# DeltaNet side tasks: order edges behind the latest dense unit, longer pauses behind loads and powers

## The chip, the cores and the metric

The kernel runs on one core of one Trainium2 chip. The metric is the device time of one execution in microseconds, as the median of several runs. The core has five engines that run side by side, each through its own list of instructions in order: TensorE (PE in the profile, its weight loads PEld), VectorE (DVE), ScalarE (ACT), GpSimd (POOL) and SyncE (SP), which issues most of the DMAs.

## The reference

A trunk of two layers on 528 tokens (16 meta tokens and 512 others) of width 1024: forgetting attention, a convolutional feed-forward block, gated DeltaNet, and a second feed-forward block. The change touches DeltaNet alone. Cut to what matters:

```python
def gated_deltanet(h, w_in, conv_w, a_log, dt_bias, o_gain, w_out):
    proj = hp @ w_in
    qkv, og, b_logit, a_logit = jnp.split(proj, ...)
    qkv = jax.nn.silu(causal_dwconv(qkv, conv_w))
    q = l2norm(q) * (Dh ** -0.5); k = l2norm(k)
    beta = jax.nn.sigmoid(b_logit)
    gc = jnp.cumsum(g, axis=-1)                      # per chunk
    dec = jnp.exp(gc[..., :, None] - gc[..., None, :])   # lower triangle
    A = jnp.where(strict, (k k^T) * dec * beta, 0.0)
    sol = triangular_solve(A + I, [k * beta * exp(gc), v * beta])
    W, U0 = sol
    qk = (q k^T) * dec
    def step(S, xs):                                 # over the chunks
        U = U0_n - W_n S
        O = qd_n S + qk_n U
        S = gl_n * S + U^T kd_n
        return S, O
    O = rmsnorm(O, o_gain) * jax.nn.silu(og)
    return O @ w_out
```

8 heads of 128 elements; the kernel uses chunks of 16, 128, 128, 128 and 128 tokens.

## The kernel before

**Dense units.** Every weight matrix is cut into units of 128 output columns. `dense` (L297 to L318) multiplies one unit with one of two halves of the tokens (272 and 256), in three products per 128 input rows (high and low parts of both sides): 24 matmuls for a unit of 1024 rows, all on L312. `push` runs the second half of a unit four units later. After its matmuls a unit has its own work on other engines: `conv_tile` takes the sums off PSUM on DVE (L748), convolves on DVE and ACT (L755, L764); `og` does the gate (L1388, L1390); `part` copies a partial output (L871).

**Tasks.** Around the dense units DeltaNet runs its recurrence in groups of two heads (g = 0 to 3). Each group has generator tasks: `kchain` makes the decays (`decays`, L1044: DVE on a row `gcr` that SP loads), the Gram matrices of K (`gram_k`: sums L1020 and products L1075 on PE, a power on POOL L1063, the matrix AT by DVE L1082), the small inverse of the first chunk (`solve_meta`, L1129), and `solve`. `solve` sends AT through DRAM (`dA`, `AB`), does 31 steps of substitution on POOL (L1177 and L1178 per step, on the tile RB), sends the result through DRAM again (`dR`, then `Rc`), and finishes the inverse with copies (L1192), a transposition (L1189) and small matmuls (L1199 to L1236). `qchain` does the same for Q. `schain` runs `scan`, chunk by chunk: transposes (L1256, L1257) and K·S (L1260) on PE, VB (ACT L1262, DVE L1265), inverse times VB (PE L1270), U (ACT L1272), U times KD (PE L1277), the new state S (DVE L1281 or L1283), and the output (PE L1289, L1291; ACT L1296, L1297). `heads_out` then norms the output: MO on DVE (L1308), a power on POOL (L1309), OU times MO on POOL (L1312), transposes on PE (L1316), and the copy to O.

**What sets the order.** `Flow` keeps a planned time `now`, which `dense` moves on by 0.33 for every three matmuls; a task that yields a number sleeps for that much planned time, one that yields a condition until it holds. `tick`, called inside `dense`, steps the tasks that are due. So the constants T_... set where a task's instructions stand among the dense matmuls. PE keeps that order for the dense matmuls and for those of `scan` (`tok`); what stands where on DVE, ACT and POOL is decided by a scheduler with its own estimates. Before a new K, Q or V tile `hd_tile` looks whether 16 of them are in use; if so, `flow.until` steps tasks until a scan has freed six, and no dense matmul is recorded meanwhile. In program order this falls 595 dense matmuls behind the first transpose of L952 (the start of the tasks); the last unit of DeltaNet ends at 1549. At the end `flow.until` runs the tasks that are left. A group's `decays` wait for the scan of the group two before; its `solve` waits for the substitution of the group before.

Of the kernel before, what the change touches and what calls it, by code (L numbers as in the profile page):

```python
# [9 lines left out]
F32 = mybir.dt.float32  # L10
# [3 lines left out]
ALU = mybir.AluOpType  # L14
# [19 lines left out]
T_BLOCKS = 4  # L34
T_STEP = 0.5
T_INV = 10
T_OUT = 3.5
# [67 lines left out]
def trunk(ctx, tc, h0, wflat, params, out):  # L105
# [110 lines left out]
    class Flow:  # L216
# [11 lines left out]
        def step(self, t):  # L228
            self.busy = True
            try:  # L230
                r = next(t["gen"])
            except StopIteration:
                self.tasks.remove(t)
                r = None
            self.busy = False
            t["cond"] = None
            if callable(r):
                t["cond"] = r
            elif r is not None:
                t["wake"] = self.now + r  # L240
# [496 lines left out]
    def conv_tile(u, half, ft, taps, base, stride, pool, carry):  # L737
# [4 lines left out]
        with tc.high_priority(offset=300):  # L742
# [5 lines left out]
            nc.vector.tensor_tensor(ub[:, c0:c0 + n], ps, r[:, :n], op=ALU.mult)  # L748
# [6 lines left out]
            nc.scalar.activation(cv, ub[:, c0:c0 + n], AF.Identity, scale=w[c0])  # L755
# [85 lines left out]
    def deltanet(layer, post, pre, wcx):  # L841
# [21 lines left out]
        def part(u, half, mt):  # L863
            n = HALF[half][1] - (CUT if half == 0 else 0)
            if mt == 0:
                drop(*X[half][:2])
                m[half] = take(half, "m", shape=[P, KT, n])
                OHL[half] = split(half, 0)
            x = OHL[half]
            ps = dense(u, half, lambda k: x[:, 0, k, :], lambda k: x[:, 1, k, :], 0, n)  # L870
            nc.vector.tensor_copy(m[half][:, mt, :], ps)  # L871
            if mt == 7:
                drop(x)
                OHL[half] = None

        with ExitStack() as cx:
# [3 lines left out]
            flow.on = False  # L880
        HALF[0] = (CUT, 272 - CUT)
# [17 lines left out]
    def dn_heads(layer, O, cx, part):  # L899
# [81 lines left out]
        def group(g):  # L981
# [47 lines left out]
            def decays(half):  # L1029
                s, n = HALF[half]  # L1030
                if half == 0:
# [4 lines left out]
                    st["QDm"] = dp.tile([16, NG, 16], F32, name="QDm", tag="QDm", bufs=2)  # L1036
                for hl in range(NG):
                    hd = g * NG + hl
                    gcr = dp.tile([P, 272], F32, name="gcr", tag="gc", bufs=2)
                    nc.sync.dma_start(gcr[:, :n], gcd[hd:hd + 1, s:s + n].to_broadcast([P, n]))  # L1040
# [11 lines left out]
            def gram_k(half):  # L1052
# [10 lines left out]
                nc.gpsimd.tensor_tensor(rk[:, cs, :], y[:, cs, :], mhalf[:, 0:w * NG].rearrange("p (c x) -> p c x", x=NG), op=ALU.pow)  # L1063
                nc.vector.tensor_tensor(rho[:, cs, :], y[:, cs, :], rk[:, cs, :], op=ALU.mult)
# [19 lines left out]
            def gram_q(half):  # L1084
# [9 lines left out]
                yield T_HOP  # L1094
                pgs = [psum_tile("g") for _ in range(NG)]
# [5 lines left out]
                for hl in range(NG):  # L1101
# [6 lines left out]
                    eg = dp.tile([P, 272], F32, name="eg", tag="gc", bufs=2)  # L1108
                    nc.sync.dma_start(eg[:, :n], gcd[hd:hd + 1, s:s + n].to_broadcast([P, n]))
# [45 lines left out]
            def solve():  # L1155
# [18 lines left out]
                for l in range(31):  # L1174
# [3 lines left out]
                    nc.gpsimd.tensor_tensor(R3[:, 0:a, l + 1:32], R3[:, 0:a, l + 1:32], t, op=ALU.subtract)  # L1178
# [125 lines left out]
            def heads_out(ci, OU, MO):  # L1304
# [8 lines left out]
                yield 0.0  # L1313
# [24 lines left out]
            def kchain(half):  # L1338
                yield lambda: ("gates", half) in done and (g < 2 or ("scan", g - 2) in done)
                decays(half)  # L1340
# [40 lines left out]
        def og(u, half, hd):  # L1381
# [98 lines left out]
```

## Time and profile before

| | |
|---|---|
| median of 3 runs | 1604.69 us (1602.89 to 1607.8) |
| the profiled execution's own time | 1601.35 us |
| its span (first to last instruction) | 1599.4 us |
| busy in the span | PE 95%, DVE 70%, ACT 51%, POOL 31% |
| mean granted TensorE clock | 0.977 |

The profile's span leaves 1.95 us of the execution outside it. Busy shares are over the whole kernel; the change touches the stretch from about 825 to 1172 us, in which PE runs dense units and tasks in turn.

### The profile page before, as it was taken

The numbers are of one execution on the slowest core, as the hardware profiler recorded it, in microseconds if no ns is written. First come the engines' busy times: TensorE is split into PE (matmuls) and PEld (weight loads), VectorE is DVE, ScalarE is ACT, GpSimd is POOL, SyncE is SP. The second block draws the span as 40 slices with busy tenths as digits, with TensorE's granted clock in tenths as the row PEclk, the third lists the DMA queues.
The fourth block names the chain that finished last, engine by engine and source line by source line (L and its number), as shares of the span: only waits on it lengthen the run. The fifth ranks groups of instructions, "written<-read, shape, count | busy, mean of one in ns | idle before, by whom it ended". The sixth has DMA issues, their size and how long they took to land.

```text
span 1599.4 us, 33295 instructions
## 1 busy us (share of the span) xinstructions
PE 1525.8 (95%) x12630; PEld 1486.8 (93%) x12630; DVE 1123.4 (70%) x2629; ACT 815.4 (51%) x1925; POOL 495.8 (31%) x993
## 2 busy tenths in 40 slices
PE   8999999999999999999789899899989999999996
PEld 6999999899999999999789798898989999999996
DVE  7888888948974675674978665676569864765764
ACT  6677777735643442343564456545456543432441
POOL 6434443025300010012556475654154200100112
PEclk9999999999999999999799998999999999999998
DMA  5232222422223222222323322222141323323321
GB/s 175 89 89 79 75 78 85 134 65 82 84 83 100 93 85 88 93 93 72 107 75 90 90 61 71 68 77 61 50 150 66 91 82 106 92 82 106 93 67 53
DMA packets 63327, 139.04 MB, mean 87 GB/s; under 512 B 18584, under 2 KB 31288, under 8 KB 62784
## 3 DMA queue, kind: packets, MB, share of 16 engines
q1 hardware_dynamic: 62544, 134.55, 28.1%
q8 instruction: 99, 1.62, 0.4%
q0 software_dynamic: 480, 2.15, 0.4%
q14 instruction: 60, 0.49, 0.1%
q10 hardware_dynamic: 144, 0.22, 0.0%
HBM read 131.54 MB, written 5.36 MB: 86 GB/s over the span
## 4 chain that ended last, share of the span: by engine, by line
PE 74%; DVE 11%; POOL 5%; DMA 4%; ACT 3%; issue 3%; SPq 1%; POOLq 0%; DVEq 0%; ACTq 0%
PE ps L312 65%; POOL PR L1177 2%; POOL RB L1178 2%; DVE h L412 1%; DVE bt L411 1%; DVE wl L292 1%; PE av L698 1%; DMA w<-wflat 1%; DVE cv L764 1%; DMA gcr<-gcd 1%; PE pt L678 1%; DVE xl L378 1%; ACT wh L285 1%; PE s L1277 1%; DVE qr L577 1%
## 5 line engine op out<-in xcount | busy, mean ns | idle before, releaser
L312 PE MATMUL ps<-xh,wh 128*128 128x256 f32 (+4 forms) x2464 | 717.6, 293 | 16.8 <-DVE ub L748 9.2
L312 PE MATMUL ps<-xl,wh 128*128 128x256 f32 (+4 forms) x2464 | 710.8, 289 | 3.4 <-DVE xl L378 3.0
L312 PE MATMUL ps<-xh,wl 128*128 128x256 f32 (+4 forms) x2464 | 713.6, 290 | 0.0
L312 PEld LDWEIGHTS ps<-xh,wh 128*128 128x128 f32 (+1 forms) x2464 | 469.6, 192 | 22.8 <-DVE ub L748 6.3
L312 PEld LDWEIGHTS ps<-xl,wh 128*128 128x128 f32 (+1 forms) x2464 | 471.1, 191 | 7.4 <-DVE xl L378 4.6
L312 PEld LDWEIGHTS ps<-xh,wl 128*128 128x128 f32 (+1 forms) x2464 | 471.1, 191 | 1.0
L285 ACT CAST wh<-w 128x1024 fp32r<-128x1024 f32 (+3 forms) x226 | 225.1, 997 | 189.5 <-PE ps L312 166.7
L292 DVE TENSOR_TENSOR wl<-w,wh 128x1024 fp32r<-128x1024 f32 (+4 forms) x191 | 220.6, 1156 | 99.3 <-ACT wh L285 98.7
L764 DVE SCALAR_TENSOR_TENSOR cv<-ub,prm,cv 128x256 f32<-128x256 f32 (+2 forms) x494 | 243.8, 498 | 38.4 <-ACT cv L755 29.5
L312 PE MATMUL ps<-ah,wl 128*128 128x256 f32 (+2 forms) x704 | 199.5, 284 | 0.0
L312 PE MATMUL ps<-ah,wh 128*128 128x256 f32 (+2 forms) x704 | 199.3, 283 | 0.0
L312 PE MATMUL ps<-al,wh 128*128 128x256 f32 (+2 forms) x704 | 199.1, 283 | 0.0
L755 ACT ACTIVATE cv<-ub,prm 128x256 f32<-128x256 f32 (+2 forms) x224 | 113.8, 511 | 146.3 <-DVE ub L748 146.2
L748 DVE TENSOR_TENSOR ub<-ps,r 128x256 f32<-128x256 f32 (+2 forms) x224 | 95.4, 428 | 101.5 <-PE ps L312 100.6
L353 POOL TENSOR_TENSOR ssq<-ssq,sq 128x256 f32<-128x256 f32 (+2 forms) x98 | 90.5, 926 | 144.5 <-ACT sq L352 143.0
L312 PEld LDWEIGHTS ps<-ah,wh 128*128 128x128 f32 x704 | 132.6, 189 | 0.0
L312 PEld LDWEIGHTS ps<-al,wh 128*128 128x128 f32 x704 | 132.5, 188 | 0.0
L312 PEld LDWEIGHTS ps<-ah,wl 128*128 128x128 f32 x704 | 132.4, 188 | 0.0
L751 POOL COPY cy<-ub 128x2 f32<-128x2 f32 (+1 forms) x112 | 38.0, 341 | 279.3 <-DVE ub L748 277.7
L292 POOL TENSOR_TENSOR wl<-w,wh 128x512 fp32r<-128x512 f32 x70 | 95.0, 1377 | 72.1 <-ACT wh L285 56.8
L747 POOL COPY ub<-cy 128x2 f32<-128x2 f32 (+1 forms) x112 | 31.3, 280 | 197.1 <-DVE cv L764 160.0
L786 ACT ACTIVATE gl<-cv 128x272 f32<-128x272 f32 (+2 forms) x88 | 36.7, 418 | 42.0 <-DVE cv L764 41.7
(308 smaller groups left out, 2454.5 us busy)
## 6 DMA issues: line engine op xcount, KB each, us to landing
w<-wflat SPq DMA_DIRECT2D x176, 512.0 KB, 3.5
w<-wflat SPq DMA_DIRECT2D x32, 448.0 KB, 3.3
cB<-cdram SPq DMA_DIRECT2D x16, 264.0 KB, 3.3
w<-wflat SPq DMA_DIRECT2D x16, 256.0 KB, 2.7
h<-h SPq DMA_DIRECT2D x8, 272.0 KB, 5.3
cB<-cdram SPq DMA_DIRECT2D x16, 136.0 KB, 3.0
h<-h SPq DMA_DIRECT2D x8, 256.0 KB, 5.0
AB<-dA SPq DMA_DIRECT2D x16, 128.0 KB, 3.2
```

The source lines that it names most:

```text
L285: nc.scalar.copy(wh[:], w32)
L292: eng.tensor_tensor(wl[:, c], w32[:, c], wh[:, c].bitcast(F32), op=ALU.subtract)
L312: tok(nc.tensor.matmul(o, w[:, a], r[:, c0:c1], start=(i == 0), stop=(i == tot - 1)))
L353: nc.gpsimd.tensor_tensor(self.acc[:, :n], self.acc[:, :n], sq[:, :n], op=ALU.add)
L747: nc.gpsimd.tensor_copy(ub[:, 0:c0], carry.pop(ft)[:, :c0])
L748: nc.vector.tensor_tensor(ub[:, c0:c0 + n], ps, r[:, :n], op=ALU.mult)
L751: nc.gpsimd.tensor_copy(c[:, :c0], ub[:, n:n + c0])
L755: nc.scalar.activation(cv, ub[:, c0:c0 + n], AF.Identity, scale=w[c0])
L764: nc.vector.scalar_tensor_tensor(cv, ub[:, i:i + n], w[i], cv, op0=ALU.mult, op1=ALU.add)
L786: nc.scalar.activation(g, cv, AF.Gelu_apprx_tanh)
L1177: nc.gpsimd.tensor_tensor(t, R3[:, 0:a, l:l + 1].to_broadcast([P, a, w]), A3[:, l:l + 1, l + 1:32].to_broadcast([P, a, w]), op=ALU.mult)
L1178: nc.gpsimd.tensor_tensor(R3[:, 0:a, l + 1:32], R3[:, 0:a, l + 1:32], t, op=ALU.subtract)
```

## The change

A dictionary `anchors` keeps, for an engine, the latest instruction of a dense unit (DVE L748, L871, L1388; ACT L755, L1390) and the latest subtraction of the substitution (POOL L1178). While a task is stepped, each instruction that it records gets an edge behind the anchor of its engine. The constants are set anew: a pause T_LOAD stands between the loads of `gcr` or `eg` and their use, T_POW behind the power of `gram_k`, T_BACK between the load of `Rc` and its first use; T_BLOCKS, T_STEP, T_INV and T_OUT have other values, and `heads_out` pauses T_OUT + 1 before its transposes in place of 0.

```diff
-T_BLOCKS = 4
-T_STEP = 0.5
-T_INV = 10
-T_OUT = 3.5
+T_BLOCKS = 8
+T_LOAD = 3.5
+T_POW = 2
+T_STEP = 0.9
+T_BACK = 5.5
+T_INV = 2.5
+T_OUT = 2
...
         def step(self, t):
             self.busy = True
-            try:
-                r = next(t["gen"])
-            except StopIteration:
-                self.tasks.remove(t)
-                r = None
+            with ExitStack() as es:
+                for i in anchors.values():
+                    es.enter_context(tc.issue_after(i))
+                try:
+                    r = next(t["gen"])
+                except StopIteration:
+                    self.tasks.remove(t)
+                    r = None
...
+    anchors = {}
+
+    def anchor(engine, inst):
+        if flow.on:
+            anchors[engine] = inst.ins
...
-            nc.vector.tensor_tensor(ub[:, c0:c0 + n], ps, r[:, :n], op=ALU.mult)
+            anchor("dve", nc.vector.tensor_tensor(ub[:, c0:c0 + n], ps, r[:, :n], op=ALU.mult))
...
-            nc.scalar.activation(cv, ub[:, c0:c0 + n], AF.Identity, scale=w[c0])
+            anchor("act", nc.scalar.activation(cv, ub[:, c0:c0 + n], AF.Identity, scale=w[c0]))
...
+                gcrs = []
                 for hl in range(NG):
                     hd = g * NG + hl
-                    gcr = dp.tile([P, 272], F32, name="gcr", tag="gc", bufs=2)
-                    nc.sync.dma_start(gcr[:, :n], gcd[hd:hd + 1, s:s + n].to_broadcast([P, n]))
+                    gcrs.append(dp.tile([P, 272], F32, name="gcr", tag="gc", bufs=2))
+                    nc.sync.dma_start(gcrs[hl][:, :n], gcd[hd:hd + 1, s:s + n].to_broadcast([P, n]))
+                yield T_LOAD
...
                 nc.gpsimd.tensor_tensor(rk[:, cs, :], y[:, cs, :], mhalf[:, 0:w * NG]..., op=ALU.pow)
+                yield T_POW
...
-                    nc.gpsimd.tensor_tensor(R3[:, 0:a, l + 1:32], R3[:, 0:a, l + 1:32], t, op=ALU.subtract)
+                    anchor("pool", nc.gpsimd.tensor_tensor(R3[:, 0:a, l + 1:32], R3[:, 0:a, l + 1:32], t, op=ALU.subtract))
                     yield T_STEP
...
                     nc.sync.dma_start(Rc[32 * b:32 * b + 32], dR[NC * b:NC * b + NC].rearrange("c j r i -> (j r) c i"))
+                yield T_BACK
                 nc.vector.transpose(Tc[:].rearrange("p c i -> p (c i)"), Rc[:].rearrange("p c i -> p (c i)"))
...
-                yield 0.0
+                yield T_OUT + 1
                 pt = psum_tile("t")
```

The same loads and pause stand in `gram_q` for `eg`; the copy of L871, the product of L1388 and the tanh of L1390 are anchored too.

What this does to the order is shown at three places. Line numbers of the changed kernel are 14 to 27 higher (L312 is L326 there, L1256 to L1291 are L1283 to L1318, L1309 is L1336, L1316 is L1343).

The first is on PE, where `hd_tile` waits for the scan of group 0, 595 dense matmuls into the tasks (s and o are tiles of the scan, t of `heads_out`, ps of the dense units). Before, the output of its chunk 2:

```order
L1277 MATMUL s<-U,KD 128x128
L1289 MATMUL o<-S,hd 128x128
L1291 MATMUL o<-U,ATQD_11250 128x128
L1289 MATMUL o<-S,hd 128x128
L1291 MATMUL o<-U,ATQD_11250 128x128
L312 MATMUL ps<-xh_10425,wh 128x272
L312 MATMUL ps<-xl_10426,wh 128x272
L312 MATMUL ps<-xh_10425,wl 128x272
```

Here 18 dense matmuls follow before the scan's next chunk, and chunks 0 to 3 all stand between dense matmuls. Now, in its chunk 2, behind the output of chunk 1:

```order
L1283 MATMUL s<-ident,hd 128x128
L1284 MATMUL s<-ident,hd 128x128
L1287 MATMUL s<-S,hd 128x128
L1297 MATMUL s<-VB,ATQD_11250 128x128
L1343 MATMUL t<-ident,OU 128x128
L1297 MATMUL s<-VB,ATQD_11250 128x128
L1304 MATMUL s<-U,KD 128x128
L1343 MATMUL t<-ident,OU 128x128
L1304 MATMUL s<-U,KD 128x128
L1316 MATMUL o<-S,hd 128x128
L1318 MATMUL o<-U,ATQD_11250 128x128
```

Chunks 1, 2, 3 and 4 of this scan now stand one behind the other with no dense matmul among them (54 matmuls and transposes of the scan, 16 small ones of `solve`), and seven transposes t of `heads_out`, for the chunk before, stand inside them. The same happens at the end of DeltaNet to chunk 3 of the last scan, and the last chunk's t stands right behind its o, where 40 dense matmuls stood between.

The second is on POOL, in the substitution of group 1 (PR, RB), where the power and the product of `heads_out` (MO, OU) stand for chunk 0 of group 0. Before, in step 11 of 31:

```order
L1177 TENSOR_TENSOR PR<-RB,AB 128x66
L1178 TENSOR_TENSOR RB<-RB,PR 128x3x22
L1309 TENSOR_TENSOR MO<-MO,mhalf 16x2
L1177 TENSOR_TENSOR PR<-RB,AB 128x63
L1312 TENSOR_SCALAR OU<-OU,MO 16x128 x2
L747 COPY ub<-cy 128x3
L1178 TENSOR_TENSOR RB<-RB,PR 128x3x21
```

And now in step 28, with chunk 1 behind the last step:

```order
L1336 TENSOR_TENSOR MO<-MO,mhalf 16x2
L1204 TENSOR_TENSOR RB<-RB,PR 128x7x4
L1339 TENSOR_SCALAR OU<-OU,MO 16x128 x2
L1203 TENSOR_TENSOR PR<-RB,AB 128x24
```

```order
L1203 TENSOR_TENSOR PR<-RB,AB 128x8
L1204 TENSOR_TENSOR RB<-RB,PR 128x8
L1234 MEMSET TM 32x8x32
L1336 TENSOR_TENSOR MO<-MO,mhalf 128x2
L1188 MEMSET RB 128x256
L1339 TENSOR_SCALAR OU<-OU,MO 128x128 x2
```

The power of chunk 0 has moved by 17 steps, and the product of chunk 1 stands behind the clearing of RB for the next group, which needs the DMA from RB to have landed.

The third is on DVE, at its first use of the tile Rc of group 0 (Wm is a tile of `solve_meta`, cv, ub and wl are of the dense units). Before:

```order
L748 TENSOR_TENSOR ub<-ps,r 128x256
L764 SCALAR_TENSOR_TENSOR cv<-ub,prm,cv 128x272
L1192 COPY ATQD_11250<-Rc 32x8x32 x2
L1064 TENSOR_TENSOR rho<-y,rk 128x4
L764 SCALAR_TENSOR_TENSOR cv<-ub,prm,cv 128x272
L292 TENSOR_TENSOR wl<-w_12379,wh 128x1024
L1189 STREAM_TRANSPOSE Tc<-Rc 128x256
L1065 TENSOR_SCALAR rk<-rk 128x4
L1148 TENSOR_TENSOR Wm<-l,Wm 16x32
```

And now:

```order
L1422 SCALAR_TENSOR_TENSOR o_12382<-ot,oz 128x260
L778 SCALAR_TENSOR_TENSOR cv<-ub,prm,cv 128x256 x3
L1415 TENSOR_TENSOR oz<-ps,r 128x260
L1216 STREAM_TRANSPOSE Tc<-Rc 128x256
L1219 COPY ATQD_11250<-Rc 32x8x32 x2
L762 TENSOR_TENSOR ub<-ps,r 128x256
L1013 SCALAR_TENSOR_TENSOR hd<-th,cv 128x256
L1235 COPY TM<-Tc 32x8x32
L306 TENSOR_TENSOR wl<-w_12612,wh 128x1024
```

The uses of Rc now stand behind more of the dense units' work and no Wm stands behind them; in the program the first small matmuls of `solve` (L1199) are now 495 dense matmuls into the tasks, where they were at 394. For the later groups they are at 595 (583 before), 1014 (874) and 1311 (1153). The last products of `gram_k` of group 1 are at 427 (345), those of group 2 at 676 to 688 (511 to 565), and those of group 3 at 952 to 979 (799 to 904).

## Rows read from the trace of the kernel before

**Rows 1.** Busy us by stretch: PE, PEld, DVE, ACT, POOL; then PEclk, DMA

```profile
825.40:1172.00 346.60, 326.90 (x2932) 308.59 (x2931) 227.10 (x635) 180.81 (x526) 177.00 (x427) 0.95 0.28 75
900.70:907.50 6.80, 4.70 (x23) 4.37 (x23) 6.42 (x21) 3.09 (x6) 2.38 (x4) 0.50 0.31 84
975.80:986.00 10.20, 10.20 (x51) 8.31 (x51) 2.09 (x8) 2.69 (x10) 3.37 (x11) 0.50 0.39 100
1027.00:1030.40 3.40, 3.15 (x15) 3.07 (x16) 2.62 (x9) 3.04 (x10) 0.00 (x0) 0.50 0.22 45
1088.40:1091.90 3.50, 3.50 (x19) 3.50 (x19) 1.58 (x4) 1.82 (x3) 1.92 (x9) 0.51 0.00 0
```

**Rows 2.** Waits of PE from 825.4 to 1172: total us, times, longest

```profile
PE l L1129 <- DVE Wm L1148: 6.1, 1, 6.1
PE t L1316 <- POOL OU L1312: 5.5, 3, 3.3
PE g L1075 <- DVE ATQD L1107: 2.8, 1, 2.8
PE s L1277 <- ACT U L1272: 1.8, 1, 1.8
PE g L1075 <- DVE y L1062: 0.9, 1, 0.9
PE ps L312 <- DVE oz L1388: 0.8, 1, 0.8
PE g L1020 <- DVE ATm L1082: 0.7, 1, 0.7
```

**Rows 3.** Timeline of DVE: start us, us, instruction, idle before and releaser

```profile
899.58 0.70 DVE L1192 COPY ATQD<-Rc 32x256 f32<-32x256 f32 x2 [7.98 <-DMA Rc<-dR]
```

**Rows 4.** Timeline of PE at three places

```profile
892.41 0.60 PE L1075 MATMUL g<-hd 128*128 128x128 f32 x4
...
902.80 0.28 PE L1129 MATMUL l<-Wm 16*16 16x16 f32 x4 [6.14 <-DVE Wm L1148]
...
963.77 0.37 PE L312 MATMUL ps<-xh,wh 128*128 128x272 f32 x1
```

**Rows 5.** Timeline of POOL, substitution of group 1 and behind it

```profile
916.17 0.24 POOL L1177 TENSOR_TENSOR PR<-RB,AB 128x31 f32<-128x31 f32 x1 [5.17 <-DMA AB<-dA]
...
950.43 0.33 POOL L1178 TENSOR_TENSOR RB<-RB,PR 128x8 f32<-128x8 f32 x1
...
950.90 0.69 POOL L1309 TENSOR_TENSOR MO<-MO,mhalf 128x2 f32<-128x2 f32 x1
...
954.81 0.31 POOL L1162 MEMSET RB<- 128x256 f32 x1 [1.48 <-DMA dR<-RB]
```

**Rows 6.** Timeline of DVE, AT and Rc of group 1

```profile
905.09 1.12 DVE L1082 SCALAR_TENSOR_TENSOR ATQD<-g,ab,ATQD 128x128 f32<-128x128 f32 x4
...
957.46 0.28 DVE L1192 COPY ATQD<-Rc 32x256 f32<-32x256 f32 x1 [4.11 <-DMA Rc<-dR]
```

**Rows 7.** Groups by line, 825.4 to 1172: busy us, mean ns, idle before

```profile
L1312 POOL TENSOR_SCALAR OU<-OU,MO 128x128 f32<-128x128 f32 (+1 forms) x40 | 26.9, 682 | 1.3
L1309 POOL TENSOR_TENSOR MO<-MO,mhalf 128x2 f32<-128x2 f32 (+1 forms) x20 | 16.2, 809 | 60.3 <-DVE MO L1308 41.4 <-PE ps L312 10.1 <-PE s L1260 8.8
L1262 ACT ACTIVATE VB<-s,rho 128x128 f32<-128x128 f32 (+1 forms) x40 | 14.0, 360 | 11.7 <-PE s L1260 10.7 <-PE s L1257 0.5
L1272 ACT ACTIVATE U<-s,ub 128x128 f32<-128x128 f32 (+1 forms) x40 | 13.0, 361 | 10.4 <-PE s L1270 10.3
L1297 ACT ACTIVATE osq<-OU 128x128 f32<-128x128 f32 (+1 forms) x40 | 12.5, 312 | 0.4
```

**Rows 8.** Dense matmuls, second feed-forward block: us, PE, PEld, PEclk

```profile
1205.00:1590.00 385.00, 377.23 (x3145) 375.49 (x3143) 1.00 0.27 82
```

**Rows 9.** Timeline at the last chunk's output, PE and POOL

```profile
1166.83 0.38 PE L1291 MATMUL o<-U,ATQD 128*128 128x128 f32 x2
...
1169.59 1.20 POOL L1312 TENSOR_SCALAR OU<-OU,MO 128x128 f32<-128x128 f32 x2
```

More of the change, by code (lines that the diff above doesn't have):

```diff
@@ L870, in part @@
             ps = dense(u, half, lambda k: x[:, 0, k, :], lambda k: x[:, 1, k, :], 0, n)
-            nc.vector.tensor_copy(m[half][:, mt, :], ps)
+            anchor("dve", nc.vector.tensor_copy(m[half][:, mt, :], ps))
             if mt == 7:
@@ L880, in deltanet @@
             flow.on = False
+            anchors.clear()
         HALF[0] = (CUT, 272 - CUT)
@@ L1036, in decays @@
                     st["QDm"] = dp.tile([16, NG, 16], F32, name="QDm", tag="QDm", bufs=2)
+                gcrs = []
                 for hl in range(NG):
                     hd = g * NG + hl
-                    gcr = dp.tile([P, 272], F32, name="gcr", tag="gc", bufs=2)
-                    nc.sync.dma_start(gcr[:, :n], gcd[hd:hd + 1, s:s + n].to_broadcast([P, n]))
+                    gcrs.append(dp.tile([P, 272], F32, name="gcr", tag="gc", bufs=2))
+                    nc.sync.dma_start(gcrs[hl][:, :n], gcd[hd:hd + 1, s:s + n].to_broadcast([P, n]))
+                yield T_LOAD
+                for hl in range(NG):
+                    hd = g * NG + hl
+                    gcr = gcrs[hl]
                     for c in CI[half]:
@@ L1094, in gram_q @@
                 yield T_HOP
+                egs = []
                 pgs = [psum_tile("g") for _ in range(NG)]
@@ L1107, in gram_q @@
                         nc.vector.scalar_tensor_tensor(d, o, col("rk")[:cn, c, hl:hl + 1], d, op0=ALU.mult, op1=ALU.mult)
-                    eg = dp.tile([P, 272], F32, name="eg", tag="gc", bufs=2)
-                    nc.sync.dma_start(eg[:, :n], gcd[hd:hd + 1, s:s + n].to_broadcast([P, n]))
+                    egs.append(dp.tile([P, 272], F32, name="eg", tag="gc", bufs=2))
+                    nc.sync.dma_start(egs[hl][:, :n], gcd[hd:hd + 1, s:s + n].to_broadcast([P, n]))
+                yield T_LOAD
+                for hl in range(NG):
+                    hd = g * NG + hl
+                    eg = egs[hl]
                     nc.scalar.activation(eg[:, :n], eg[:, :n], AF.Exp)
@@ L1339, in kchain @@
                 yield lambda: ("gates", half) in done and (g < 2 or ("scan", g - 2) in done)
-                decays(half)
+                yield from decays(half)
                 yield from gram_k(half)
@@ L1387, in og @@
             z = tmp2("oz")[:, :n]
-            nc.vector.tensor_tensor(z, ps, r[:, c], op=ALU.mult)
+            anchor("dve", nc.vector.tensor_tensor(z, ps, r[:, c], op=ALU.mult))
             th = tmp2("ot")[:, :n]
-            nc.scalar.activation(th, z, AF.Tanh, scale=0.5)
+            anchor("act", nc.scalar.activation(th, z, AF.Tanh, scale=0.5))
             o = O[half][:, hd, c]
```

## The prediction

> **What bounds the kernel now.** I read first the busy shares, then PE's waits in the stretch that the change touches, then the granted clock by stretch, and last the timelines around each wait, to see what stood in front of the instruction that was waited for. PE bounds the kernel: in the 346.6 us from the first task to the last it is busy for 326.9 [rows 1]. So only two things can change the time: stretches in which PE stands, and stretches in which it works at the lower clock. PE's waits there sum to 18.6 us: 6.1, 5.5 (three transposes of `heads_out` that wait for POOL), 2.8, 1.8, 0.9, 0.8 and 0.7 [rows 2]. The largest shows the pattern. PE waits 6.14 us for Wm on DVE [rows 4]; on DVE the copies of Rc stand in front, idle for 7.98 us until the DMA has landed at 899.58 [rows 3]. An engine's list is served in order, so a wait for a DMA holds whatever is behind it. The clock comes on top. From 900.7 to 907.5, right behind the long wait, the granted clock is 0.50, that is 1.2 GHz for 2.4; so it is for 3.4 us behind the waits of 1018 to 1027 and again behind that of 1085 [rows 1]. At half clock half of the time is lost if PE is busy.
>
> **What the change removes.** The uses of Rc now stand 5.5 planned us behind their load and behind the next dense work; Tc's first matmuls are 101 dense matmuls later for group 0, about 12 us at 385 / 3145 = 0.122 us each [rows 8]. That ends the waits of 6.1 and 1.8 and, at group 2, the 2.8. The pauses behind the power and the loads give the 0.9, 0.8 and 0.7 room, with dense matmuls as cover; if that cover were gone they would be back, 2.4 us in all. Together 13.1 us. Of the 5.5 us of transposes that wait for POOL I keep 2.5: the planner's order edge only sets how early MO may stand on POOL, and in the substitutions of groups 2 and 3 it still stands at steps 10, 21, 30 and 31. The bounds are 0 (PE comes later, since it runs slower) and 5.5 (as now). That saves 3.0. Of the lower clock the stretch behind 900.7 goes (6.8 / 2 = 3.4) and the one of 1027 (3.4 / 2 = 1.7): 5.1; the one behind 1085 I keep with its wait, the 10.2 us from 975.8 have no wait of PE in front of them, so they stay too [rows 1]. Saved: 13.1 + 3.0 + 5.1 = 21.2 us.
>
> **What it adds: the scan of group 0.** Since the chain of tasks starts later, the scan of group 0 begins at 556 dense matmuls, and at 595 `hd_tile` lets nothing dense in before it is over. Chunks 1 to 4 then have no cover.
> When does PE get there? Before, it is there at 963.8 [rows 4]. Less the work that now stands behind this point (three chunks at 24 passes of 0.11 us, 2.65 each, and six transposes: 8.8; group 2's Gram sums and products, 40 passes: 4.5; other small matmuls 1.1; 14.4 in all), less the waits up to there (6.1 + 1.8 + 0.9 + 0.8 + 0.7 = 10.3) and the clock's 3.4: about 936.
> When is POOL ready? Inside chunk 1 stands the transpose of chunk 0's OU, which POOL now multiplies in step 28 of group 1's substitution. That starts when AB has landed. Before, the products of K ended at 892.4 + 0.6 but DVE, held by Rc, made AT only until 906.2 [rows 4, 6], and POOL began at 916.17 [rows 5]. Now the products stand 82 dense matmuls later: 10.0 us, plus 3 of other PE work, less the waits of 0.9 and 0.7: 904.4; with 1.4 for DVE again about 906. So what DVE lost before, the later place takes now, and POOL begins at 916 either way. It took 34.6 us until 950.76 [rows 5]; of that 4.8 were two powers of `gram_k` and chunk 1's MO and OU, which now stand elsewhere. The end, S, is about 946.5 and step 28 at 944. PE stands from 936 or 937 to 944.
> Then: chunk 1's OU stands behind the clearing of RB, which comes when dR has landed, 950.76 to 954.81 = 4.05 us behind S, and takes 0.3 [rows 5]; two products of 0.68 [rows 7] bring its transposes to S + 5.8. What is left of chunk 2 ends at about S + 7; its state stands on DVE behind the copies of Rc, which came 957.46 - 950.76 = 6.7 behind S [rows 5, 6], so S + 8. Chunks 3 and 4 have five hops each; ACT alone does VB, KD, U, two copies and squares with a read for two heads, 0.36 and 0.31 the longer ones [rows 7], some 3.7 us, and with the hops 5 us a chunk. The dense matmuls go on at S + 18 = 964.5. The stretch is 28.5 us long, and PE's own rows in it are 54 of the scan at about 0.2, seven transposes and 16 small ones, 11.8. Added: 16.7 us. The bounds are 10 (POOL 7 us earlier, so that PE does not stand for step 28) and 21 (each PE hop at the lower clock).
> Behind the 6.14 us wait the clock was low for 6.8 us; part of that falls into the stretch here, and I add one of 3.4 us behind it, 1.7. The Trainium skill, "TensorE: Matmul & The Clock Gate", section "HAM oscillation — how this bites in real kernels", says that bursts of matmuls between waits start at the lower clock each time. By the row I add 1.7; by that rule, as an estimate, all 11.8 us of PE's rows would run at 1.2 GHz, and the sum would be up to 10 us higher; the trace agrees in that the low stretches follow the waits.
>
> **What it adds: the end.** In the last scan the rest of chunk 3 is bare: its MO follows its chunk 2 by too little, about 1.6 us of standing. The last transposes now stand right behind the last o. Before, that o ended at 1167.2 and OU at 1170.8 [rows 9]: 3.6 us that 40 dense matmuls hid, less 0.2 for the transposes of chunk 3. Added 5.0, and one low stretch of 3.4 us, 1.7. The bounds are 3 and 8.
>
> **The sum.** Added 16.7 + 1.7 + 5.0 + 1.7 = 25.1, saved 21.2: +4 us on the profiled execution's 1601.35 (span 1599.4), so 1605.3. The median of the runs shown is 1604.69, 3.3 above; on it the sum is 1608.7. A measurement of this kernel tells no change from a change of under 0.3%, 4.8 us, so the forecast is no change, at its slow edge.
>
> **The rivals.**
> *Faster: POOL is not late.* If PE keeps its full clock up to group 1's Gram products (901.8), if the way through DRAM takes 8 us and the substitution 29, S is 940 and PE hardly stands for step 28: 6.8 off; PE then also finds the later transposes ready (2.5) and the clock up (3.4): 4 - 12.7 = -8.7, 1596. For it: DVE no longer stands at 892 to 899. Against it: the place of the products on PE is a floor, and the chain through POOL and DRAM is as long as before.
> *Slower: the clock.* If PE runs the bare stretch at 1.2 GHz throughout, its twelve hops (three a chunk) each take 0.3 longer, 3.6, and the dense work behind starts with a low stretch of 10.2 us in place of 3.4, as at 975.8, 3.4 more: 4 + 7 = +11, 1615.7. This decides if the clock falls with the first standing at 937 and does not come back before the stretch is over. For it: behind the one wait of 6.14 us it stayed at 0.50 for 6.8 us, though PE had work again from 902.8 [rows 1, 4]. Against it: the other two low stretches behind waits lasted 3.4 us only [rows 1].
> That the edges do nothing is excluded: the order shows the rows moved. That the removed waits stay is, too, for the two at Rc.
>
> **How the numbers follow.** No change 0.40 (its own range 1600 to 1609.5), slower 0.38, faster 0.22. The range is 1596 to 1620: the faster case's own time, and the slower one's with 4 for the upper bounds of the transposes and the end.
>
> **What would show it.** Right: no wait of PE for Wm nor for U behind Rc; PE idle or at 0.5 for most of some 28 us in one place around 935 to 965, with waits of PE's t for POOL's OU and of VB, U, S; POOL's substitution of group 1 beginning at 916 and ending at 946 or 947; about 4 us of PE standing just ahead of the out projection. Wrong: POOL's group 1 starting before 910, or that stretch under 20 us (then faster), or the clock at 0.5 for over 20 us in a row (then slower); or PE waits in the scans of groups 1 to 3, which I have at 2.5 us.

## The result and the profile after

Median of 20 executions each: 1603.53 us before, 1608.32 us after; the ratio is 1.0031, with a 95% interval of 1.0017 to 1.0045. The forecast was 1608.7 and "no change, at its slow edge". The change costs about 5 us. That it costs something is clear of the noise; whether it is more than the 0.3% that the forecast took for no change is not, since the interval lies on both sides of it.

The page of the changed kernel, its span and PE:

```profile
span 1607.0 us, 33302 instructions
PE 1530.5 (95%) x12630; PEld 1491.4 (93%) x12630; DVE 1122.0 (70%) x2628; ACT 811.2 (50%) x1920; POOL 487.8 (30%) x993
```

The span is 7.6 us longer than before's 1599.4, the mean granted clock 0.973 (0.977). The waits of PE from the first task to the last transpose of `heads_out`, which answer to [rows 2] (total us, times, longest):

```profile
PE t L1343 <- POOL OU L1339: 12.7, 5, 4.4
PE s L1297 <- ACT KD L1293: 5.1, 5, 1.6
PE l L1155 <- DVE Wm L1170: 3.0, 1, 3.0
PE ps L326 <- DVE ub L762: 0.6, 1, 0.6
PE g L1096 <- DVE ATQD L1103: 0.5, 1, 0.5
```

The transposes that wait for POOL went from 5.5 to 12.7 us; KD (K with its decays, made by ACT for the scan), which was not in the list, has 5.1. The wait for Wm has halved, those behind `gram_k`'s DVE work and behind Rc are nearly gone. The stretches, as in [rows 1] (PE, PEld, DVE, ACT, POOL busy; PEclk; DMA): the tasks, the wait for Wm, the bare scan of group 0, the wait at group 2, the end.

```profile
825.40:1176.30 350.90, 327.57 (x2950) 308.95 (x2949) 226.94 (x635) 179.97 (x527) 171.46 (x428) 0.95 0.28 74
889.40:898.70 9.30, 6.29 (x33) 6.19 (x32) 5.22 (x14) 2.38 (x7) 4.16 (x21) 0.63 0.60 148
940.70:970.50 29.80, 19.88 (x132) 17.63 (x131) 9.78 (x31) 13.91 (x53) 15.19 (x44) 0.71 0.17 36
1025.40:1031.80 6.40, 3.05 (x15) 3.03 (x15) 2.75 (x5) 1.77 (x4) 5.86 (x14) 0.74 0.38 93
1172.30:1199.10 26.80, 22.28 (x160) 21.79 (x160) 13.87 (x28) 13.77 (x31) 14.27 (x20) 0.87 0.57 174
```

In the third row PE is busy for 19.9 of 29.8 us, at 0.71: idle 9.9 us, and at 0.50 for 17.1. I count such a stretch as **lost time**: PE's idle time (neither a matmul nor a weight load runs) plus half of the time in which it works at the low clock. Of the 17.1 us 4.6 are idle too, so the stretch loses 9.9 + (17.1 - 4.6) / 2 = 16.1 us. Counted in that way over the whole span, before loses 100.6 us and after 109.0, and what is left is 1498.8 and 1498.0: idle and clock are the whole difference, to less than 1 us. In all fourteen profiles of this study the span less the lost time lies between 1497.0 and 1502.0. So the table below gives what each profiled execution loses between 815 and 1300 us, where the tasks and their end are; outside it before loses 49.2 us and after 51.0, with the same work.

The bare scan in the timeline of the changed kernel (start us, us, instruction, idle before and releaser), as in [rows 4, 5]: POOL's substitution of group 1, and PE.

```profile
916.23 0.43 DVE L1216 STREAM_TRANSPOSE Tc<-Rc 128x256 f32<-128x256 f32 x1
...
921.03 0.24 POOL L1203 TENSOR_TENSOR PR<-RB,AB 128x31 f32<-128x31 f32 x1 [4.71 <-DMA AB<-dA]
...
947.84 1.20 POOL L1339 TENSOR_SCALAR OU<-OU,MO 16x128 f32<-16x128 f32 x2
...
950.50 0.21 POOL L1204 TENSOR_TENSOR RB<-RB,PR 128x8 f32<-128x8 f32 x1
...
948.50 0.28 PE L1343 MATMUL t<-ident,OU 16*128 16x16 f32 x1 [4.39 <-POOL OU L1339]
...
970.54 0.36 PE L326 MATMUL ps<-xh,wh 128*128 128x256 f32 x1
```

PE asks for chunk 0's OU at 944.1, POOL multiplies it in step 28 of the substitution at 947.84, and the next dense matmul is at 970.54. The end, as in [rows 9]:

```profile
1174.56 1.19 POOL L1339 TENSOR_SCALAR OU<-OU,MO 128x128 f32<-128x128 f32 x2
...
1175.22 1.06 PE L1343 MATMUL t<-ident,OU 128*128 128x128 f32 x2 [2.92 <-POOL OU L1339]
```

### The profile page after: what moved, and what is told of

Its sections match the earlier page's. It is cut to its first block, busy times and chain, and to the rows that moved or that the text cites. A ratio compares the mean times of both kernels' runs of the same rounds, so it can differ in the third digit from the quotient of the medians.

```text
span 1607.0 us, 33302 instructions
## 1 busy us (share of the span) xinstructions
PE 1530.5 (95%) x12630; PEld 1491.4 (93%) x12630; DVE 1122.0 (70%) x2628; ACT 811.2 (50%) x1920; POOL 487.8 (30%) x993
## 4 chain that ended last, share of the span: by engine, by line
PE 73%; DVE 10%; POOL 6%; issue 4%; ACT 3%; DMA 3%; SPq 1%; POOLq 0%; DVEq 0%; ACTq 0%
PE ps L326 64%; POOL PR L1203 2%; POOL RB L1204 2%; DVE bt L425 1%; DVE h L426 1%; PE av L712 1%; DMA w<-wflat 1%; DVE wl L306 1%; DVE xl L392 1%; PE pt L692 1%; DVE cv L778 1%; DMA AB<-dA 1%; DVE qr L591 1%; PE g L1035 1%; PE sc L660 1%
## 5 line engine op out<-in xcount | busy, mean ns | idle before, releaser
L326 PE MATMUL ps<-xh,wh 128*128 128x256 f32 (+4 forms) x2464 | 715.6, 292 | 17.0 <-DVE ub L762 10.2
L326 PE MATMUL ps<-xl,wh 128*128 128x256 f32 (+4 forms) x2464 | 710.2, 289 | 2.8 <-DVE xl L392 2.4
L326 PE MATMUL ps<-xh,wl 128*128 128x256 f32 (+4 forms) x2464 | 712.7, 290 | 0.0
L326 PEld LDWEIGHTS ps<-xh,wh 128*128 128x128 f32 (+1 forms) x2464 | 469.6, 191 | 22.4 <-DVE ub L762 7.2
L326 PEld LDWEIGHTS ps<-xl,wh 128*128 128x128 f32 (+1 forms) x2464 | 469.7, 191 | 6.2 <-DVE xl L392 3.7
L326 PEld LDWEIGHTS ps<-xh,wl 128*128 128x128 f32 (+1 forms) x2464 | 469.6, 191 | 1.3
L326 PE MATMUL ps<-ah,wl 128*128 128x256 f32 (+2 forms) x704 | 199.5, 284 | 0.0
L326 PE MATMUL ps<-ah,wh 128*128 128x256 f32 (+2 forms) x704 | 199.3, 283 | 0.0
L326 PE MATMUL ps<-al,wh 128*128 128x256 f32 (+2 forms) x704 | 199.1, 283 | 0.0
L326 PEld LDWEIGHTS ps<-ah,wh 128*128 128x128 f32 x704 | 132.6, 189 | 0.0
L326 PEld LDWEIGHTS ps<-al,wh 128*128 128x128 f32 x704 | 132.5, 188 | 0.0
L326 PEld LDWEIGHTS ps<-ah,wl 128*128 128x128 f32 x704 | 132.4, 188 | 0.0
L761 POOL COPY ub<-cy 128x2 f32<-128x2 f32 (+1 forms) x112 | 29.8, 266 | 208.5 <-DVE cv L778 169.6
```

The lines of the kernel that those rows point to most:

```text
L326: tok(nc.tensor.matmul(o, w[:, a], r[:, c0:c1], start=(i == 0), stop=(i == tot - 1)))
L761: nc.gpsimd.tensor_copy(ub[:, 0:c0], carry.pop(ft)[:, :c0])
```

## The experiments

Ratios are to the kernel before, measured beside each run; its medians there lay between 1600.58 and 1604.44 us, so kernels are compared by their ratios. Idle, low (time at 0.50) and lost are us from 815 to 1300 of the profiled execution. That is one execution, and not always a typical one: e1's took 1605.79 us and e4's 1615.97, beside medians of 1602.15 and 1613.67. So the three columns say where an execution lost its time, and not by how much two kernels differ.

| kernel | median us | ratio (95%) | idle | low | lost |
|---|---|---|---|---|---|
| before | 1603.53 | | 30.7 | 47.8 | 51.4 |
| after | 1608.32 | 1.0031 (1.0017 to 1.0045) | 35.4 | 54.6 | 58.0 |
| e1 before + edges | 1602.15 | 0.9988 (0.9976 to 1.0001) | 31.1 | 54.6 | 56.3 |
| e2 after, no edges | 1620.05 | 1.0097 (1.0081 to 1.0112) | 41.7 | 64.9 | 67.1 |
| e3 after, T_STEP 0.5 | 1604.78 | 1.0000 (0.9989 to 1.0011) | 35.1 | 47.8 | 55.3 |
| e4 after, GL on ACT | 1613.67 | 1.0052 (1.0032 to 1.0072) | 37.9 | 68.3 | 65.8 |
| e5 e4 + two RB | 1605.31 | 1.0024 (1.0009 to 1.0039) | 31.2 | 51.2 | 53.6 |
| e6 after, H1 ahead of K3 | 1616.85 | 1.0100 (1.0079 to 1.0121) | 32.4 | 74.6 | 66.5 |
| e7 before + T_BACK | 1602.04 | 1.0001 (0.9984 to 1.0018) | 28.5 | 58.0 | 54.2 |
| e8 mix | 1610.62 | 1.0058 (1.0038 to 1.0077) | 34.8 | 51.2 | 57.4 |
| e9 e5 with T_STEP 0.65 | 1604.44 | 1.0009 (0.9994 to 1.0024) | 30.5 | 47.8 | 51.9 |
| e10 e5 with T_STEP 0.5 | 1608.39 | 1.0030 (1.0014 to 1.0046) | 35.2 | 58.0 | 60.8 |
| e11 e1 + two RB | 1601.39 | 0.9991 (0.9976 to 1.0006) | 33.5 | 44.4 | 51.9 |
| e12 e11 + pauses | 1602.61 | 1.0001 (0.9986 to 1.0015) | 31.9 | 47.8 | 53.3 |

**e1, the edges alone; e2, the constants alone.** e1 adds the anchors and the edges of `step` to the kernel before. e2 takes them out of the changed kernel:

```diff
     def anchor(engine, inst):
-        if flow.on:
-            anchors[engine] = inst.ins
+        pass
```

> The kernel before with the order edges alone: the anchors of DVE, ACT and POOL, and no constant and no pause changed. My theory is that the change gains and loses by its constants (where the uses of Rc and the scan of group 0 stand), not by the edges: so within 3 us of before (1600.5 to 1606.5), with DVE still held for some 5 to 8 us by the load of Rc of group 0, and no stretch at 595 dense matmuls in which PE runs no dense matmul for more than 10 us. The rival is that the edges themselves cost, since they hold DVE, ACT and POOL behind the latest dense unit: then it is as slow as the changed kernel, 1607 to 1611, with its waits spread over many tiles.

> The changed kernel without any order edge; its constants and pauses stay. My theory (the constants make the time): within 3 us of the changed kernel's 1608.3, with the bare stretch at 595 dense matmuls still there (94 small matmuls and transposes in a row on PE by the order, 77 with the edges), some 28 us long, and PE standing in it for 9 us or more. The rival (the edges cost): 1600 to 1605, back at the kernel before.

e1's time came out as I expected, but not the hold that I expected with it. For group 0 DVE no longer stands for Rc: its copy, in front of which DVE was idle for 7.98 us in the kernel before [rows 3], has no idle time in front of it, and PE's wait for Wm there is 1.2 us. What is left of the hold in e1 is in the later groups.

```profile
894.70 0.27 DVE L1202 COPY ATQD<-Rc 32x256 f32<-32x256 f32 x1
```

e2 fits neither theory: its 1.0097 is 0.66%, some 11 us, more than with the edges. The hold by Rc is back, larger than ever. Idle time until the load of Rc has landed, of DVE and ACT together, 820 to 1172 us (us, times), in the view of the tile Rc, for before, e1, after and e2:

```profile
  DMA Rc<-dR: 27.1, 6
```

```profile
  DMA Rc<-dR: 21.5, 7
```

```profile
  DMA Rc<-dR: 3.5, 3
```

```profile
  DMA Rc<-dR: 43.5, 10
```

In the timeline of e2 DVE stands for the load that the changed kernel finds landed at 916.23:

```profile
900.49 0.28 DVE L1218 COPY ATQD<-Rc 32x256 f32<-32x256 f32 x1 [7.60 <-DMA Rc<-dR]
```

PE's three longest waits in e2 from 880 us on (6.0 us until 902.3, 5.0 until 1033.3 and 3.8 until 1109.7) each end less than 2 us behind the start of a copy of Rc for which DVE and ACT had stood.

So most of the hold goes only with both halves together. Without an edge the scheduler of DVE's list puts the copies ahead of the dense work that the pause let through; without the longer constants the edge is enough for group 0, and in the later groups it holds the copies behind dense work that is not far enough on (DVE stands 5.0 us at 951 in e1). In time the edges alone are the better kernel: 0.9988, and 1.0031 with both.

**e3, the place of the scan.**

```diff
-T_STEP = 0.9
+T_STEP = 0.5
```

> The changed kernel with T_STEP at 0.5 as before, all else kept. By the order the scan of group 0 then begins 105 dense matmuls earlier (its first chunk at 469 in place of 574), the row of matmuls with nothing dense among them at 595 shrinks from 77 to 29, and the last scan's chunk 3 has its cover again; the first matmuls on Tc stand at 410 in place of 495. My theory: the place at 595 gives back 10 to 15 us and the end 4, while the hold of DVE by Rc comes back with 6 us of PE's wait and 3.4 us of lower clock's loss: 1608.3 - 16 + 9.5 = 1602, between 1597 and 1605. The rival (PE stands wherever POOL is late, so the place does not matter): 1606 to 1611, with the t waits moved and as long as now, 12.7 us in all.

1604.78, 1.0000, as expected by the theory; against the changed kernel's 1.0031 it gives back 0.3%. The lost time shows it smaller (55.3 for 58.0), since PE still waits at transposes and, behind a DVE that stands for gcr, at Wm:

```profile
PE t L1343 <- POOL OU L1339: 10.9, 4, 4.0
...
PE l L1155 <- DVE Wm L1170: 2.4, 1, 2.4
```

So the rival was right in one point: the transposes wait for POOL nearly as long (10.9 for 12.7) wherever the scan stands.

**e4 and e5, the wait for Wm that stayed.** The changed kernel's timeline has its cause: POOL copies GL (each chunk's last decay) from eg (the row of decays that SP loads for Q) in the substitution, SP's load of gcr into the same buffer goes out behind that, DVE stands for gcr, and Wm behind it.

```profile
886.82 0.19 POOL L1139 COPY GL<-eg 128x2 f32<-128x2 f32 x1
...
887.03 0.80 SPq L1056 DMA_DIRECT2D gcr<-gcd  x2
...
890.63 1.29 DVE L1064 SCALAR_TENSOR_TENSOR ATQD<-gcr,COL,dmask 128x128 f32<-128x128 f32 x4 [5.87 <-DMA gcr<-gcd]
...
892.47 0.28 PE L1155 MATMUL l<-Wm 16*16 16x16 f32 x4 [3.02 <-DVE Wm L1170]
```

e4 moves the copy, e5 gives RB a second buffer besides:

```diff
-                    nc.gpsimd.tensor_copy(GL[:, hd, c0:c0 + 2], eg[:, o + 127:n:128])
+                    nc.scalar.copy(GL[:, hd, c0:c0 + 2], eg[:, o + 127:n:128])
...
-                RB = dp.tile([P, 256], F32, name="RB", tag="RB")
+                RB = dp.tile([P, 256], F32, name="RB", tag="RB", bufs=2)
```

> The changed kernel with one instruction moved: the copy of GL from eg, on ACT in place of POOL, where an order edge keeps it behind the latest subtraction of the substitution. In the changed kernel PE waits 3.0 us at 889.5 for Wm; DVE in front of it is idle for 5.87 us until gcr has landed at 890.6, whose load SP issued at 887.0, after POOL had made the copies of GL at 886.8 to 887.4 although eg was ready at 880. My theory: with the copy on ACT the load goes out some 5 us earlier, the 3.0 us are gone, and the low clock behind (891.9 to 898.7, 3.4 us lost) with it: 3 to 6 us faster, 1602 to 1605.5, POOL's group 1 starting before 919 in place of 921.0. The rival: the 3 us are only waited for later, at the transpose that waits for POOL's product in the substitution of group 1, since the substitution's end does not move: within 1.5 us of 1608.3.

> The run before, with the copy of GL on ACT, showed the wait for Wm not gone but moved: PE waits 4.99 us at 896.8 for Wm; DVE in front is idle for 9.06 us behind the tanh of ACT, ACT for 9.65 us behind a product of a dense unit on POOL (cv, L780), and POOL stood 4.12 us at its clearing of RB, until dR<-RB had landed. So here RB has two buffers besides, and the clearing needs no DMA. My theory: it is a chain of lists held by DMAs, and with both holds gone PE's wait for Wm is gone (under 0.5 us in all between 880 and 905) and the transposes of chunk 1 in the bare stretch no longer stand behind the clearing (0.8 us): 1608.3 - 3.0 - 0.8 and 1 to 3.4 of lower clock, 1601 to 1604. The rival: what is not waited for at Wm is waited for at the bare stretch, where PE needs POOL's step 28 at about 948: its wait there grows from 4.4 to 7 us, and the time stays at 1606.5 to 1610.

e4's time missed both: 1613.67, where the theory had at most 1605.5 and the rival 1609.8. In e4 gcr lands in time and PE waits longer than in the changed kernel, since another list is held by another DMA. The timeline of e4, from POOL's clearing over a dense unit's product to PE:

```profile
898.87 0.31 POOL L1188 MEMSET RB<- 128x256 f32 x1 [4.12 <-DMA dR<-RB]
...
900.77 0.43 ACT L1010 ACTIVATE th<-cv 128x272 f32<-128x272 f32 x1 [9.65 <-POOL cv L780]
...
901.23 0.44 DVE L1013 SCALAR_TENSOR_TENSOR hd<-th,cv 128x272 f32<-128x272 f32 x1 [9.06 <-ACT th L1010]
...
901.82 0.28 PE L1155 MATMUL l<-Wm 16*16 16x16 f32 x4 [4.99 <-DVE Wm L1174]
```

With RB doubled too (e5) the wait is 0.8 us (I had under 0.5) and the idle time 4 us less than in the changed kernel, so the chain of held lists is shown. What the rival named, a longer wait at the bare scan, did not come: 3.98 us there, 4.39 in the changed kernel. POOL and PE just come to it 4 to 6 us earlier, as the timeline of e5 has it for the first row of the substitution, the product in step 28, PE's transpose that waits for it, and the first dense matmul behind the scan:

```profile
916.90 0.26 POOL L1203 TENSOR_TENSOR PR<-RB,AB 128x31 f32<-128x31 f32 x1 [4.45 <-DMA AB<-dA]
...
944.17 1.20 POOL L1339 TENSOR_SCALAR OU<-OU,MO 16x128 f32<-16x128 f32 x2
...
944.84 0.29 PE L1343 MATMUL t<-ident,OU 16*128 16x16 f32 x1 [3.98 <-POOL OU L1339]
...
964.83 0.36 PE L326 MATMUL ps<-xh,wh 128*128 128x256 f32 x1
```

In e4, where the wait for Wm is longer, POOL comes to that first row later:

```profile
923.47 0.49 POOL L1203 TENSOR_TENSOR PR<-RB,AB 128x31 f32<-128x31 f32 x1 [4.25 <-DMA AB<-dA]
```

So with waits for Wm of 0.8, 3.0 and 5.0 us (e5, the changed kernel, e4) the substitution begins at 916.9, 921.0 and 923.5. e5's time, 1605.31 and 1.0024, lies between theory and rival and is not told apart from the changed kernel's 1.0031. Nor is e4's 1.0052, whose interval overlaps with it. What e4's profile loses more (65.8 us for 58.0) is mostly clock: its low time is 13.7 us longer, and its six executions ran from 1607.0 at a mean clock of 0.976 to 1616.8 at 0.971.

**e6, the wall moved.** Only the order of the dense units changes:

```diff
-... H0 Q2 K3 V2 H1 Q3 ...
+... H0 Q2 H1 K3 V2 Q3 ...
```

> The changed kernel with the dense units in another order: the units of the gates H1 stand ahead of K3 in place of behind V2, so that the 16th tile hd is asked for 96 dense matmuls later. By the order the row of matmuls with nothing dense among them goes from 77 at 595 to 52 at 691; the one at the end, at 1519, from 22 to 46. My theory (what is bare costs, wherever): PE stands 3 to 5 us less at the first place, the wait of 4.4 us for chunk 0's OU gone, since dense matmuls stand there now, and 4 to 6 us more at the end: 1605 to 1611, no gain. The rival (the place is all of the loss, the end is cheap): 1600 to 1604.

1616.85: both fell. The idle time is 3 us less in all (32.4 for 35.4). At the first place, between 940 and 975 us, it is 6.8 us for 9.9, as expected, though PE still waits 3.2 us there for chunk 0's OU, a wait that I had as gone; from 1150 us on it is 2.3 us more, where I had 4 to 6. But the low time rose from 54.6 to 74.6 us. 23.9 us of it lie between 980 and 1025, where PE does not stand at all. Two stretches of e6 from there:

```profile
985.00:999.00 14.00, 14.00 (x68) 11.87 (x68) 6.80 (x27) 6.32 (x18) 3.91 (x5) 0.51 0.08 23
1009.00:1019.00 10.00, 10.00 (x53) 9.24 (x53) 3.11 (x13) 2.90 (x12) 5.63 (x18) 0.50 0.27 73
```

**e7, the pause alone**, in the kernel before:

```diff
-T_INV = 10
+T_BACK = 5.5
+T_INV = 4.5
...
+                yield T_BACK
                 nc.vector.transpose(Tc[:]..., Rc[:]...)
```

> The kernel before with one part of the change: the pause T_BACK of 5.5 behind the load of Rc; T_INV goes from 10 to 4.5, so that the first matmuls on Tc stay where they are (393 dense matmuls into the tasks). My theory: a pause that doesn't move PE's own use saves little. Tc is there at 902.3 in the kernel before, and PE, which now does not wait for Wm, comes to its matmuls on Tc at about 898 and waits there for 3 to 5 us: 1600 to 1604.5, under 0.3% from before. The rival, which my prediction's sum comes near to (the hold of DVE is the loss): the 6.1 and 1.8 us and 3.4 of lower clock go: 1590 to 1596.

No change, 1.0001, as expected, but for another reason: PE does not come to Tc. The pause, with no edge, does not take DVE's hold away (DVE and ACT stand 30.0 us for Rc in all, 27.1 in the kernel before), and the wait for Wm is as in [rows 2, 3]:

```profile
897.77 0.28 DVE L1194 COPY ATQD<-Rc 32x256 f32<-32x256 f32 x1 [7.59 <-DMA Rc<-dR]
...
901.04 0.29 PE L1130 MATMUL l<-Wm 16*16 16x16 f32 x4 [6.95 <-DVE Wm L1149]
```

**e8 to e12, towards a better kernel.** e8 is before with the edges, T_BACK 5.5 and T_INV 4.5, GL on ACT, two RB and H1 ahead of K3; e9 and e10 are e5 with T_STEP 0.65 and 0.5; e11 is e1 with two RB; e12 is e11 with T_BACK 5.5 and T_INV 4.5, a pause of 4 in `heads_out` ahead of its transposes, and three buffers of OU.

> What the runs so far speak for, on the kernel before: the order edges (0.9988 alone), T_BACK 5.5 with T_INV 4.5, the copy of GL on ACT, two buffers of RB, and H1 ahead of K3. No constant is longer than before in sum, so no scan is bare: the longest row without a dense matmul has 54, at 406, of which 16 are on Tc and 24 on M and Rc. My theory: the holds by gcr and by the clearing of RB are gone, the clearing no longer in front of chunk 1's product: 3 to 8 us below before, 1596 to 1601. The rival: POOL's substitution sets the time at which the scan of group 0 can go on, and PE stands at Tc or at the first transposes of heads_out instead: 1602 to 1606.

> The changed kernel with T_STEP at 0.65 in place of 0.9, GL on ACT and two buffers of RB. In the changed kernel Rc of group 0 has landed at about 900 and its first use stands at 916.2, so the chain of tasks was put some 16 us later than the data ask for; with T_STEP 0.5 that use came at 901.8, as soon as Rc was there. By the order the first matmuls on Tc stand at 410 dense matmuls (495 changed), the longest row without a dense matmul is 36, at 595 (77), and the end is covered again. My theory (how far the chain is late is the loss, and the holds by gcr and RB are a loss of their own): idle PE from 815 us to the last transpose of heads_out falls from the changed kernel's 23.3 us to 17 to 20, and the time to 1599 to 1603 or 0.996 to 1.001 of before. The rival: the lower clock takes it back, as it did with GL on ACT alone (27.3 us lost at half clock in that stretch, 19.3 in the changed kernel): 1604 to 1609.

> The run with T_STEP 0.5, now with GL on ACT and two buffers of RB besides. That run had PE idle for 22.3 us from 815 to the last transpose, 2.4 of it for Wm behind gcr and 10.9 at transposes that wait for POOL. My theory: the 2.4 go and 1 to 2 of the transposes, 1 to 4 us faster than that run's 1.0000 of before: 0.9975 to 0.9995. The rival: POOL's product is late by the place of the substitution and not by the clearing, and the clock scatters by more than is saved: 0.9990 to 1.0030.

> The kernel before with the order edges and two buffers of RB. With the edges alone (0.9988 of before) POOL's clearing of RB stood 3.7 us for dR<-RB at 888 to 891.8 and 4.9 us at 943 to 947.8; 4.2 us of PE's 19.3 idle us stand at 947.8 for KD. My theory: what POOL and, behind it, ACT and DVE hold there is gone, 2 to 5 us of idle PE less: 0.9955 to 0.9985 of before. The rival: these holds are off the path here, the same 0.9988, between 0.998 and 1.001.

> The kernel before with the order edges, two buffers of RB, T_BACK 5.5 with T_INV 4.5, and a pause of 4 (before 0) ahead of the transposes of heads_out, with three buffers of OU for it. With the edges and two buffers of RB alone, PE was idle for 24.4 us from 815 us to the last of these transposes: 8.0 of it at transposes that wait for POOL's product, 5.0 for KD behind ACT's copies of Rc (3.8 at one place, at 951.5, where ACT stood 4.5 us for Rc). By the order the transposes stand 18 to 70 dense matmuls later, and the end stays covered. My theory (a use that stands behind its producer's real time costs PE nothing, and edges and pause together set it): the transposes wait 2 to 4 us in place of 8.0, KD under 2 in place of 5.0, idle 16 to 19 us, and the time 0.994 to 0.998 of before. The rival: the waits only change their names, since POOL's chain of substitutions is what PE comes too early for, and the time stays at 0.998 to 1.002.

None beats the kernel before by more than can be told. e8 missed by 10 us; which of its parts did it was not taken apart (H1 ahead of K3 is in e6 too, and slow there). e9's ratio lies in the theory's range and its time, 1604.44, in the rival's; its idle time up to the last transpose is 22.0 us, where I had 17 to 20. e10 came out at the upper edge of its rival. e9 and e10 have the wait for Wm back (4.4 and 4.5 us), since with a shorter T_STEP the uses of Rc stand in front of it again; DVE in e9:

```profile
902.73 0.28 DVE L1219 COPY ATQD<-Rc 32x256 f32<-32x256 f32 x1 [9.72 <-DMA Rc<-dR]
```

e11 and e12 went as their rivals: the clearing of RB was off the path in e1, and in e12, behind a pause of 4, the transposes still wait 7.1 us (8.0 in e11), for POOL's product, most of it at the same three places (about 931, 1025 and 1092 us). The longest wait for KD in e11, 3.8 of 5.0 us, has its hold in ACT's timeline; it is what the pauses shortened (2.0 in e12):

```profile
954.50 0.40 ACT L1202 COPY ATQD<-Rc 32x256 f32<-32x256 f32 x1 [4.51 <-DMA Rc<-dR]
```

## Why the prediction was right, step by step

**What bounds it** held: idle PE and the low clock are the whole difference between the spans.

**The sum** held to some 3 us, with its terms off in both directions. Measured by lost time between 815 and 1300 us: the bare scan loses 16.1 us (forecast 16.7 + 1.7); the end, 1160 to 1199.1, loses 8.9, where before loses 0.4 up to 1191.4, so 8.5 (forecast 5.0 + 1.7); the rest is 58.0 - 16.1 - 8.9 = 33.0 for before's 51.4 - 0.4 = 51.0, so 18.0 are saved (forecast 21.2). Net +6.6; the forecast was +4. The profiled spans differ by 7.6, the medians by 4.8. That the forecast of 1608.7 lies 0.4 us from the median is luck: it stands on a median of three that was 1.2 us above that of twenty, single executions of the changed kernel lie up to 9 us apart, and one term that was off, the low clock from 975.8, differs from profile to profile.

**What is saved.** The uses of Rc hold DVE and ACT for 3.5 us in place of 27.1, and the waits for U and at group 2's products are gone: right, and e1, e2 and e7 show that for the whole of it the edge and the later place are needed together. That no wait for Wm would be left was wrong. The step that failed is "That ends the waits of 6.1": the wait is 3.0 us. I looked only at what stood in front of Wm before. A load of gcr, held by a POOL copy that the new POOL edge keeps in the substitution, took the place; the stretch from 889.4 to 900 still loses 6.1 us with its low clock, where before's from 896 to 908 loses 8.5. The lower clock behind 1027 stayed too. What made up for it I had written off: the 10.2 us at low clock from 975.8 [rows 1], 5.1 lost, are not there in this profile. That is not shown to be the change's doing: 10.2 us at low clock stand at this place in e5 (976.0 to 986.2) and in e10 (980.5 to 990.7), which have the change too.

**Transposes.** Of 5.5 us I kept 2.5 for groups 2 and 3, and more than that was one of my signs of being wrong. They are 3.4 and 1.2 us, and behind the first the clock falls: from 1025 to 1033 the kernel loses 4.9 us. The order edge did not bring MO nearer to its use. In e3 and e12 these waits are 10.9 and 7.1 us, with another T_STEP and another pause; that they follow POOL's substitutions is what this speaks for, not shown by a run that takes the product off POOL.

**The bare scan.** The mechanism, its place and its length (29.8 us for 28.5) were right; every time in it is 4 to 8 us later than forecast. POOL began group 1 at 921.0 (916), the product of step 28 let PE go on at 948.5 (944), the substitution ended at 950.7 (946.5), PE stood for it from 944.1 (936), the dense matmuls went on at 970.5 (964.5). The cause is the wait for Wm that I had counted as gone, with the low clock behind it: in e5, where 0.8 us of it is left, POOL begins at 916.9, PE goes on at 944.8 and the dense matmuls at 964.8, within 1 us of the forecast's 916, 944 and 964.5. Since PE and POOL came late together, the standing was no longer. PE stood less for step 28 (4.4 us for 7 to 8), as it was there at 940.9 even in e5 and not at 936, and lost more by the clock: 17.1 us of the stretch at 0.50, where I had one stretch of 3.4 behind it. So the term came out by two errors: 9.9 us idle where I had 16.7, and 6.2 by the clock where I had 1.7. The Trainium skill, "TensorE: Matmul & The Clock Gate", section "HAM oscillation — how this bites in real kernels", tells of a kernel whose bursts of matmuls start at 1.2 GHz each time, behind DMA waits of 3 to 5 us. I had left out how long those waits are. Here 12.5 of PE's 19.9 busy us ran at 1.2 GHz, though a single wait of the stretch, that of 4.39 us, is so long, and the first low stretch began at 943.1, ahead of it. So the trace lies between my row and all of PE's work at 1.2 GHz, nearer to the latter, and the low clock ahead of that wait is not the page's case.

**The end** was under-sized: waits of 0.8 and 2.9 us, less than the 5.0 forecast, but 1.5 more at the sums of the next norm, and two low stretches of 3.4 us in place of one.

**The rivals.** Faster wanted POOL early; it was 5 us later than in the sum. Slower wanted the clock low through the whole stretch: it was low for 57% of it, so between forecast and rival. The forecast was +4 us and the rival +11; the medians differ by 4.8 and the profiled spans by 7.6. That T_STEP 0.9 may itself be too long I saw only behind the result: Rc has landed at about 900 and is used at 916.2. e3 took most of that back, and the 0.3% with it. But e10, which adds two repairs to e3, is slower than e3, at 1.0030, with 10 us more at the low clock in its profile. Why stays open, and with it how much of the 0.3% is T_STEP's.

## What to carry to other kernels

A pause in the order of the program moves an instruction only if an edge holds it there, and an edge helps only as far as what it waits behind is late enough: look at the list of the engine, not at the program. Where a wait of an in-order list is taken away, write down what stands next in that list and which load it needs, and follow it through the engines behind (POOL, ACT, DVE, PE here): the change took Rc's hold from in front of Wm and brought out gcr's, and moving that one brought out RB's. And where the gain looked for is some us in 1600, count idle time and low clock apart: e6 had 3 us less idle time than the changed kernel and was 0.7% slower.

## What the runs showed of the hardware

I had not expected the clock to fall where PE doesn't stand, although [rows 1] has such a stretch, from 975.8, which the prediction's "the low stretches follow the waits" leaves out. The same part of the program, behind the bare scan, in the changed kernel and then in e4:

```profile
978.00:1000.00 22.00, 22.00 (x192) 19.77 (x190) 15.67 (x55) 12.23 (x39) 6.38 (x11) 1.00 0.26 69
```

```profile
980.00:1002.00 22.00, 22.00 (x114) 19.26 (x115) 9.98 (x36) 8.13 (x23) 5.25 (x9) 0.53 0.13 41
```

PE is busy for all of both; in e4 it ran at 1.2 GHz for 20.5 us, from 981.0, and got through 114 matmuls in place of 192. PE's last wait before was of 0.4 us at 969.1. By number, most of what it ran there in both kernels was small products of the tasks (76 of the 114 in e4, 134 of the 192 in the changed kernel); by time it was dense matmuls (some 17 of the 22 us in both). The fall also differs from one execution to the next: the 20 executions of the changed kernel had mean clocks from 0.968 to 0.978 and times from 1612.5 to 1604.3 us at these ends (the longest, 1613.4, at 0.974). What makes it fall was not settled; no run here varies that alone.
